# Decay and rate products of two pairs in one group on the row halves, and the first weight chunk sent in two cuts

## The chip, the cores and the metric

The kernel runs on one core of a Trainium2 chip. Its time is the device time of one execution in microseconds, the median of several runs. Engines are called as the profile calls them: PE is TensorE (PEld its weight load), DVE is VectorE, ACT is ScalarE, POOL is GpSimd, SP is SyncE, which here issues most of the DMAs.

## The reference

One trunk layer of a decoder in float32, for 256 prompt tokens and 8 sample tokens (264 columns, T in the kernel). D_MODEL is 2048, the feed-forward width 5504.

```python
x = x + 0.5 * swiglu(rmsnorm(x, n1), f1g, f1u, f1d)
proj = rmsnorm(x, nm) @ w_in            # 1536 columns of attention, 3328 of RWKV
o_att  = sliding-window attention with sinks (16 query heads, 4 key heads)
o_rwkv = rwkv_time_mix(proj[..., 1536:], ...)
x = x + concat(o_att, o_rwkv) @ w_out
x = x + 0.5 * swiglu(rmsnorm(x, n2), f2g, f2u, f2d)
y = rmsnorm(x, final_norm)

# in rwkv_time_mix; wl, al are 64 columns each of the shifted projection
w = -softplus(-(w0 + tanh(wl) @ w2)) - 0.5
logw = -exp(w)                          # decay
a = sigmoid(a0 + al @ a2)               # rate
kk = k * k_k;  k = k * (1 + (a - 1) * k_a);  kk = kk / norm(kk)
S, y = wkv_scan(S0, r, logw, k, v, kk, a)
```

## The kernel before

**Stages.** First feed-forward block (0 to 766 us of the profiled execution), mixing with the projection by `w_in` (766 to 1157), the rest of `w_out` (to 1271), second feed-forward block (to 1967), final norm.

**Weight products.** All big products go through `gemm` (L132). It walks the 128-row blocks of the inner dimension in chunks of CH = 4: `chunk` (L121) loads 128x512 float32 weights on SP into `raw` (ring of 6), copies them on ACT to `hi` (L128, a reduced float32 format, ring of 4), and subtracts on DVE into `lo` (L59 and L129, ring of 4). The activations are kept as pairs (`s`, `t`, `y`, `o`) of a high and a low part too. Three matmuls for each 128x128 block, `hi` by both parts and `lo` by the high part, 12 a chunk, add up in a PSUM tile `acc` (3 banks). All other products use PSUM tiles `m` (5 banks, `mp`, L118). With these the eight banks are taken.

**The order.** A list scheduler orders the instructions of each engine by its own model of time, inside the dependences, priorities (`tc.high_priority`) and pinned orders (`keep_in_program_order`). Between engines only semaphores order the work. Each engine works through its list in order, so an instruction that waits holds up all behind it.

**Start.** `first_ffn` (L290) loads `x0` on ACT's queue (the first 128 rows of x beside the norm gains), splits it, and asks for the first chunk of gate weights (L307) behind that split. Then come x's blocks 1 (on ACT's queue), 2 and 3 (on SP's). The first pass works chunk by chunk over eight PSUM banks.

**Mixing.** The 38 column blocks of `w_in` are produced in the order of SEQ (L38): two blocks of the low-rank inputs, then four batches of two pairs of heads, three blocks (r, k, v) to a pair; then keys and values, then queries. After each chunk, `gemm` calls `tick`, which advances each of the spawned tasks (generators) by one step. The first two blocks give `la` (128 rows: 64 of `wl`, 64 of `al`) and `sgl`, and `tw`, 65 rows: tanh of the first 64 of `la`, and a row of ones.

For each pair a task `prep` (L416) runs through: the decay product (`tw` by the pair's `ld` tile, 65 rows, the 65th carrying w0), the rate product (`la` by the other half of the `ld` tile, 128 rows of which the upper 64 are zero weights), each with its own PSUM tile `m`; Tanh of both on ACT; then Copy (`kk`) and Square on ACT; some steps later the norm product `m<-t,C`, whose result DVE inverts; a scan over the columns on DVE (L433); exponentials on ACT (`W`, `Wi`, and a short one to `XD`); and further products.

For each batch a task `chain` (the triangular solve and the passing of the state) follows: rounds of DVE instructions on `X`, `Xt` and `st`, transposes into `PT` and `TT` (L569 to L577), products `m<-PT,gm`, `m<-TT,W`, and so on; at its end each pair's output is normalised (squares, two products by `C`, a square root `t<-m,eps` on ACT, a reciprocal on DVE, L705) and gated by a product of `sgl` with another `ld` tile. ACT loads a set of function tables (ACT_TABLE_LOAD) ahead of an instruction whose function is not in the set that is loaded.

Names of tiles in profile rows: `tw`, `la`, `sgl`, `X`, `Xt`, `st`, `PT`, `TT`, `gm`, `kr`, `bk` as in the code; `ld` small loaded tiles; `t` temporaries (ring of NT = 16); `C` the constants; `vec` and `half` vectors of per-row parameters; `x`, `s` the input and its split.

Of the kernel before, what the change touches and what calls it, by code (L numbers as in the profile page):

```python
# [7 lines left out]
F32 = mybir.dt.float32  # L8
F32R = mybir.dt.float32r
AF = mybir.ActivationFunctionType  # L10
ALU = mybir.AluOpType
# [15 lines left out]
BATCH = [2, 2, 2, 2]  # L27
CH, NRAW, NHL = 4, 6, 4
NACC, NM = 3, 5
NS, NO, NY, NH, NT, NLD = 38, 8, 8, 40, 16, 6  # L30
NWARM = 11
NGM, NKR, NUV, NTT, NBT = 10, 5, 3, 2, 5
NSTEP = 4
# [6 lines left out]
PASS = [[0,1,2,3],[4,5,6,7],[8,9,10,11,12,13,14,15]]  # L40

VG1, VGM, VG2, VGF = 0, 16, 32, 48
VMU, VKK, VKA, VA0, VRK, VLW, VLB, VSK, VSD = 64, 90, 98, 106, 114, 122, 130, 138, 154
NVEC = 155
CID, CBO, CCM, CMK = 0, 128, 256, 384


def body(tc, I, O):
# [9 lines left out]
    def tt(e, out, a, b, op):  # L58
        return e.tensor_tensor(out=out, in0=a, in1=b, op=op)  # L59
# [40 lines left out]
    with ExitStack() as ctx:  # L100
# [17 lines left out]
        def mp():  # L118
            return pp.tile([P, 512], F32, tag="m", bufs=NM, name=uid("m"))

        def chunk(src, n, e, ahead=True):  # L121
            w = n * P
            with tc.high_priority() if ahead else nullcontext():
                raw = wp.tile([P, CH * P], F32, tag="raw", bufs=NRAW, name=uid("raw"))
                hi = wp.tile([P, CH * P], F32R, tag="hi", bufs=NHL, name=uid("hi"))
                lo = wp.tile([P, CH * P], F32R, tag="lo", bufs=NHL, name=uid("lo"))
                SP.dma_start(raw[:, :w], src)
                A.copy(hi[:, :w], raw[:, :w])  # L128
                tt(e, lo[:, :w], raw[:, :w], hi[:, :w].bitcast(F32), ALU.subtract)  # L129
            return hi, lo  # L130

        def gemm(ps, src, xs, step=None, rng=None, ahead=True, ready=None):  # L132
# [157 lines left out]
        def first_ffn(n2):  # L290
            def load(k0):
                return n1.split(xr[k0], True)

            def nxt(o):
                n2.split(xr[o])
                n2.square(xr[o])
                A.dma_start(xsp[o], xr[o])

            with tc.tile_pool(name="f1", bufs=1) as fp:
                cur[0] = (fp, NH)  # L300
                x0 = fp.tile([P, KD + T], F32, name="x0")
                A.dma_start(x0, I["x0"])
                n1 = Norm(VG1, gains=x0[:, 0:KD])
                xr = [x0[:, KD:]]
                at = load(0)
                with tc.issue_after(at.ins):
                    first = chunk(I["gu1"][0, 0][:, 0:CH * P], CH, V, False)  # L307
                for e, j0, j1 in ((A, 1, 2), (SP, 2, 4)):
                    xg = fp.tile([P, j1 - j0, T], F32, name=uid("x"))
                    e.dma_start(xg, I["xT"][:, j0:j1, :])  # L310
                    xr += [xg[:, j] for j in range(j1 - j0)]

                def more(q):
                    xg = fp.tile([P, 4, T], F32, tag="x", bufs=3, name=uid("x"))
                    tc.keep_in_program_order(A.dma_start(xg, I["xT"][:, q * 4:q * 4 + 4, :]))
                    xr.extend(xg[:, j] for j in range(4))

                ffn(n1, xr, I["gu1"], I["dn1"], nxt, load, more, None, first)
# [27 lines left out]
        def mixing_body(mx, n2, n3, XD, XR):  # L346
            def fix(shape, name):
                return mx.tile(list(shape), F32, name=name)
# [13 lines left out]
            G.memset(keep.rearrange("p (c t) -> p c t", c=4)[:, :, 0:1], 0.0)  # L362
            shc = fix((P, NSH, NB + 1), "shc")
            wc = fix((P, NPAIR, 4), "wc")
            tw = fix((65, T), "tw")
            G.memset(tw[64:65, :], 1.0)
            rs = fix((P, T), "rs")
            PJ = [fix((P, 268), f"pj{i}") for i in range(3)]
            for pj in PJ:
# [2 lines left out]
            unit = fix((P, 32), "unit")  # L372
            for i in range(4):
                G.tensor_copy(unit[i * 32:i * 32 + 32, :], ident[i * 32:i * 32 + 32, i * 32:i * 32 + 32])
            half = fix((P, 16), "half")
            ts(V, half, vec[:, VKA:VKA + 16], 0.5, ALU.mult)
            less = fix((P, 8), "less")
            ts(V, less, half[:, 0:8], -1.0, ALU.mult, 1.0, ALU.add)
            mu = vec[:, VMU:VMU + NSH]
# [32 lines left out]
            def c4(x):  # L412
                return x[:, :NP].rearrange("p (c t) -> p c t", c=4)

            def prep(p, bt, k, xrr, xk, xv):
                lw = load(I["lw"][p], (P, 256))  # L416
                zp = mp()
                mm(zp[:, :T], lw[0:65, 0:P], tw[0:65, :])
                ap = mp()
                mm(ap[:, :T], lw[:, P:2 * P], la)  # L420
                sg, a = tmp(), tmp()
                act(sg, zp[:, :T], AF.Tanh, scale=0.5)
                ts(G, sg, sg, 0.5, ALU.mult, 0.5, ALU.add)
                act(a, ap[:, :T], AF.Tanh, scale=0.5, bias=half[:, 8 + p:9 + p])
                kk, b = tmp(), tmp()
                act(kk, xk, AF.Copy, scale=vc(VKK + p))
                act(b, kk, AF.Square)
# [430 lines left out]
                odv[0] = od  # L858

            shifted(0, la)  # L860
            act(tw[0:64, :], la[0:64, :], AF.Tanh)
            shifted(1, sgl)
            act(sgl, sgl, AF.Tanh, scale=0.5)
            ts(G, sgl, sgl, 0.5, ALU.mult, 0.5, ALU.add)
# [156 lines left out]
def layout(i):  # L1021
# [3 lines left out]
    for n in (1, 2):  # L1025
# [10 lines left out]
    heads = np.array([(2 * p + h) * 4 + j for h in range(2) for p in range(2) for b in range(NB) for j in range(4)])  # L1036
    a["vec"] = c(np.concatenate([
        v(i["ffn1_norm"][0]), v(i["mix_norm"][0]), v(i["ffn2_norm"][0]), v(i["final_norm"]),
        v(i["shift_mu"][0][sc]), v(i["key_k"][0]), v(i["key_a"][0]), v(i["aaa_a0"][0]),
        v(i["bonus_r_k"][0].reshape(-1)), v(i["ln_x_w"][0]), v(i["ln_x_b"][0]),  # L1040
        np.broadcast_to(i["attn_sinks"][0], (P, 16)), i["attn_sinks"][0][heads][:, None]], 1))
    e64 = np.kron(np.eye(2), np.ones((64, 64)))
# [2 lines left out]
    a["cst"] = c(np.concatenate([np.eye(P), e64, np.eye(P) - e64 / 64,   # L1045
                                 np.concatenate([m, m], 0)], 1).astype(f4))
    a["shs"] = c(i["state_shift"][0][:, sc].reshape(NB, NSH, P).transpose(2, 1, 0))
    lw = np.zeros((8, P, 256), f4)
    lw[:, :64, :P] = i["decay_w2"][0].reshape(64, 8, P).transpose(1, 0, 2)
    lw[:, 64, :P] = i["decay_w0"][0].reshape(8, P)  # L1050
    lw[:, 64:, P:] = i["aaa_a2"][0].reshape(64, 8, P).transpose(1, 0, 2)
    a["lw"] = lw
    a["g2"] = c(i["gate_g2"][0].reshape(P, 8, P).transpose(1, 0, 2))
    bk = _buckets()
# [38 lines left out]
```

## Time and profile before

| what | value |
|---|---|
| median of 3 runs | 1982.49 us (1981.63 to 1985.6) |
| span of the profiled execution | 1978.1 us; its own time was not taken apart from the runs, which lie 4.4 us above the span by their median |
| instructions | 45244 |
| PE busy | 1962.6 us, 99% |
| DVE, ACT, POOL busy | 67%, 52%, 14% |
| DMA | 357.26 MB, mean 181 GB/s |

In the rows of the groups and of a timeline stands: the start in us (timeline only), busy time, engine, line, operation, output tile <- input tiles, shapes and types, the number of instructions taken together (x2), and in brackets the engine's idle time before and what ended it. The ends of PE's rows are modelled, so its spacing is read from starts.

### The profile page before, as it was taken

The page shows a single profiled execution, that of the slowest core. Times are in us where ns is not written, and L with a number is a line of the kernel's source. Part 1 is how long each engine was busy: PE and PEld are TensorE (multiplying, and loading weights), DVE is VectorE, ACT ScalarE, POOL GpSimd, SP SyncE. Part 2 cuts the span into 40 slices and gives each one's busy share as a digit, 9 for nine tenths or more (in the row PEclk, how much of TensorE's full clock was granted, in tenths as well). Part 3 has the DMA queues.
Part 4 walks back from the last instruction along what each step waited for, and adds up shares of the span by engine and source line. Part 5 has one row for each costly group of instructions (what it writes and reads, how often), then busy time and mean ns, then how long its engine had stood idle before and what let it go on. Part 6 is the DMA issues. An engine that isn't in the chain of part 4 may idle for free.

```text
span 1978.1 us, 45244 instructions
## 1 busy us (share of the span) xinstructions
PE 1962.6 (99%) x17011; PEld 1944.7 (98%) x17011; DVE 1318.0 (67%) x2591; ACT 1037.1 (52%) x2069; POOL 267.2 (14%) x382
## 2 busy tenths in 40 slices
PE   9999999999999999999999999999999999999998
PEld 9999999999999999999999999999999999999998
DVE  5865555655556567799988766866666666666655
ACT  5644444444444456666656754654444444444445
POOL 0401001010010113222211000210101001010012
PEclk9999999999999999999999999999999999999999
DMA  7565565655555567554545455565666566666654
GB/s 238 178 191 191 184 191 193 183 185 174 188 180 182 182 189 230 162 165 147 147 140 172 134 161 180 177 182 187 189 185 194 182 192 188 190 192 181 192 179 147
DMA packets 218875, 357.26 MB, mean 181 GB/s; under 512 B 33552, under 2 KB 72352, under 8 KB 218656
## 3 DMA queue, kind: packets, MB, share of 16 engines
q1 hardware_dynamic: 212144, 345.76, 56.1%
q10 hardware_dynamic: 6512, 8.61, 1.3%
q8 instruction: 133, 2.18, 0.4%
q14 instruction: 86, 0.70, 0.1%
HBM read 346.67 MB, written 9.69 MB: 180 GB/s over the span
## 4 chain that ended last, share of the span: by engine, by line
PE 96%; DVE 2%; DMA 1%; issue 1%; ACT 1%; SPq 0%; DVEq 0%; ACTq 0%
PE acc L75 88%; PE m L75 8%; DVE lo L59 0%; ACT t L69 0%; DMA x<-in_x 0%; DMA raw<-in_wout 0%; DVE y L59 0%; DVE st L59 0%; DVE Xt L59 0%; DMA sa<-gm 0%; DMA ld<-in_sT 0%; ACT hi L128 0%; PE m L505 0%; DVE t L705 0%; DVE gm L59 0%
## 5 line engine op out<-in xcount | busy, mean ns | idle before, releaser
L59 DVE TENSOR_TENSOR lo<-raw,hi 128x512 fp32r<-128x512 f32 (+1 forms) x1288 | 869.6, 679 | 526.9 <-ACT hi L128 504.5
L128 ACT CAST hi<-raw 128x512 fp32r<-128x512 f32 (+1 forms) x1288 | 777.4, 607 | 839.5 <-PE acc L75 766.0
L75 PE MATMUL acc<-s,hi 128*128 128x264 f32 x5940 | 1110.9, 286 | 2.3 <-DVE o L62 1.0
L75 PEld LDWEIGHTS acc<-s,hi 128*128 128x128 f32 x5940 | 923.4, 188 | 6.7 <-ACT hi L128 1.8
L75 PE MATMUL acc<-s,lo 128*128 128x264 f32 x2970 | 847.5, 286 | 0.5 <-DVE lo L59 0.5
L75 PEld LDWEIGHTS acc<-s,lo 128*128 128x128 f32 x2970 | 558.7, 188 | 2.2 <-DVE lo L59 0.9
L75 PE MATMUL acc<-t,hi 128*128 128x264 f32 x2752 | 502.8, 284 | 0.0
L75 PEld LDWEIGHTS acc<-t,hi 128*128 128x128 f32 x2752 | 426.0, 188 | 0.0
L75 PE MATMUL acc<-t,lo 128*128 128x264 f32 x1376 | 388.5, 284 | 0.0
L59 POOL TENSOR_TENSOR t<-t,t 128x264 f32<-128x264 f32 (+1 forms) x148 | 151.0, 1020 | 1146.6 <-ACT hi L128 789.4
L75 PEld LDWEIGHTS acc<-t,lo 128*128 128x128 f32 x1376 | 258.1, 188 | 0.0
L75 PE MATMUL acc<-y,hi 128*128 128x264 f32 x648 | 123.7, 284 | 0.0
L75 PEld LDWEIGHTS acc<-y,hi 128*128 128x128 f32 x648 | 101.2, 188 | 0.1
L75 PE MATMUL acc<-y,lo 128*128 128x264 f32 x324 | 91.9, 284 | 0.0
L59 DVE TENSOR_TENSOR t<-acc,t 128x264 f32<-128x264 f32 x156 | 67.4, 432 | 35.8 <-PE acc L75 35.5
L59 POOL TENSOR_TENSOR o<-o,o 128x264 f32<-128x264 f32 x43 | 35.8, 833 | 235.8 <-ACT o L69 231.8
L75 PE MATMUL acc<-o,hi 128*128 128x264 f32 x324 | 62.4, 282 | 0.0
L75 PEld LDWEIGHTS acc<-y,lo 128*128 128x128 f32 x324 | 60.8, 188 | 0.0
L69 ACT ACTIVATE t<-t 128x264 f32<-128x264 f32 (+1 forms) x110 | 46.6, 424 | 8.8 <-DVE t L433 5.5
L62 DVE SCALAR_TENSOR_TENSOR s<-acc,s 128x264 f32<-128x264 f32 x96 | 40.6, 427 | 15.5 <-PE acc L75 15.1
L75 PEld LDWEIGHTS acc<-o,hi 128*128 128x128 f32 x324 | 49.9, 188 | 0.0
L75 PE MATMUL m<-s,hi 128*128 128x264 f32 x260 | 47.9, 284 | 0.0
(261 smaller groups left out, 1283.5 us busy)
## 6 DMA issues: line engine op xcount, KB each, us to landing
raw<-in_gu SPq DMA_DIRECT2D x688, 256.0 KB, 3.3
raw<-in_dn SPq DMA_DIRECT2D x224, 256.0 KB, 2.8
raw<-in_win SPq DMA_DIRECT2D x152, 256.0 KB, 3.4
raw<-in_dn SPq DMA_DIRECT2D x160, 192.0 KB, 2.7
raw<-in_wout SPq DMA_DIRECT2D x64, 256.0 KB, 3.2
xsp<-x ACTq DMA_DIRECT2D x16, 132.0 KB, 3.4
s<-xsp SPq DMA_DIRECT2D x16, 132.0 KB, 4.0
ld<-in_sT SPq DMA_DIRECT2D x16, 128.0 KB, 2.9
```

The lines of the kernel that those rows point to most:

```text
L59: return e.tensor_tensor(out=out, in0=a, in1=b, op=op)
L62: return V.scalar_tensor_tensor(out=out, in0=a, scalar=s, in1=b, op0=op0, op1=op1)
L69: return A.activation(out=out, in_=in_, func=f, **k)
L75: return TE.matmul(out, lhsT, rhs, start=start, stop=stop, **k)
L128: A.copy(hi[:, :w], raw[:, :w])
```

## The change

- The decay and rate products of the two pairs of a batch are issued together, when the first pair's `prep` starts (`rates`). The `ld` tile of a pair is now 128x128: its upper 64 rows hold the decay weights, its lower 64 the rate weights. The decay product takes rows 0 to 63 of the array, the rate product rows 64 to 127.
- w0 no longer comes from a row of ones in `tw` (now 64 rows) but as the bias of Tanh; `vec` and `half` grow by 8 columns, and the memset of `tw`'s last row is gone.
- Each pair's Tanh outputs are kept in `bt.gates` until its `prep` takes them; the ring of `t` has 17 tiles.
- `chunk` takes cuts. For the first chunk of gate weights alone, the first 128 of 512 columns are loaded, cast and subtracted on their own, then the other 384.

```diff
--- before.py
+++ after.py
@@ -27,7 +27,7 @@
 BATCH = [2, 2, 2, 2]
 CH, NRAW, NHL = 4, 6, 4
 NACC, NM = 3, 5
-NS, NO, NY, NH, NT, NLD = 38, 8, 8, 40, 16, 6
+NS, NO, NY, NH, NT, NLD = 38, 8, 8, 40, 17, 6
 NWARM = 11
 NGM, NKR, NUV, NTT, NBT = 10, 5, 3, 2, 5
 NSTEP = 4
@@ -40,8 +40,8 @@
 PASS = [[0,1,2,3],[4,5,6,7],[8,9,10,11,12,13,14,15]]
 
 VG1, VGM, VG2, VGF = 0, 16, 32, 48
-VMU, VKK, VKA, VA0, VRK, VLW, VLB, VSK, VSD = 64, 90, 98, 106, 114, 122, 130, 138, 154
-NVEC = 155
+VMU, VKK, VKA, VA0, VW0, VRK, VLW, VLB, VSK, VSD = 64, 90, 98, 106, 114, 122, 130, 138, 146, 162
+NVEC = 163
 CID, CBO, CCM, CMK = 0, 128, 256, 384
 
 
@@ -118,15 +118,18 @@
         def mp():
             return pp.tile([P, 512], F32, tag="m", bufs=NM, name=uid("m"))
 
-        def chunk(src, n, e, ahead=True):
+        def chunk(src, n, e, ahead=True, cuts=None):
             w = n * P
+            cuts = [0, *(cuts or []), w]
             with tc.high_priority() if ahead else nullcontext():
                 raw = wp.tile([P, CH * P], F32, tag="raw", bufs=NRAW, name=uid("raw"))
                 hi = wp.tile([P, CH * P], F32R, tag="hi", bufs=NHL, name=uid("hi"))
                 lo = wp.tile([P, CH * P], F32R, tag="lo", bufs=NHL, name=uid("lo"))
-                SP.dma_start(raw[:, :w], src)
-                A.copy(hi[:, :w], raw[:, :w])
-                tt(e, lo[:, :w], raw[:, :w], hi[:, :w].bitcast(F32), ALU.subtract)
+                for c0, c1 in zip(cuts, cuts[1:]):
+                    c = slice(c0, c1)
+                    SP.dma_start(raw[:, c], src[:, c])
+                    A.copy(hi[:, c], raw[:, c])
+                    tt(e, lo[:, c], raw[:, c], hi[:, c].bitcast(F32), ALU.subtract)
             return hi, lo
 
         def gemm(ps, src, xs, step=None, rng=None, ahead=True, ready=None):
@@ -304,7 +307,7 @@
                 xr = [x0[:, KD:]]
                 at = load(0)
                 with tc.issue_after(at.ins):
-                    first = chunk(I["gu1"][0, 0][:, 0:CH * P], CH, V, False)
+                    first = chunk(I["gu1"][0, 0][:, 0:CH * P], CH, V, False, (P,))
                 for e, j0, j1 in ((A, 1, 2), (SP, 2, 4)):
                     xg = fp.tile([P, j1 - j0, T], F32, name=uid("x"))
                     e.dma_start(xg, I["xT"][:, j0:j1, :])
@@ -362,8 +365,7 @@
             G.memset(keep.rearrange("p (c t) -> p c t", c=4)[:, :, 0:1], 0.0)
             shc = fix((P, NSH, NB + 1), "shc")
             wc = fix((P, NPAIR, 4), "wc")
-            tw = fix((65, T), "tw")
-            G.memset(tw[64:65, :], 1.0)
+            tw = fix((64, T), "tw")
             rs = fix((P, T), "rs")
             PJ = [fix((P, 268), f"pj{i}") for i in range(3)]
             for pj in PJ:
@@ -372,8 +374,8 @@
             unit = fix((P, 32), "unit")
             for i in range(4):
                 G.tensor_copy(unit[i * 32:i * 32 + 32, :], ident[i * 32:i * 32 + 32, i * 32:i * 32 + 32])
-            half = fix((P, 16), "half")
-            ts(V, half, vec[:, VKA:VKA + 16], 0.5, ALU.mult)
+            half = fix((P, 24), "half")
+            ts(V, half, vec[:, VKA:VKA + 24], 0.5, ALU.mult)
             less = fix((P, 8), "less")
             ts(V, less, half[:, 0:8], -1.0, ALU.mult, 1.0, ALU.add)
             mu = vec[:, VMU:VMU + NSH]
@@ -412,16 +414,26 @@
             def c4(x):
                 return x[:, :NP].rearrange("p (c t) -> p c t", c=4)
 
+            def rates(p0, n):
+                ws = [load(I["lw"][p0 + j], (P, P)) for j in range(n)]
+                pre = [(mp(), mp()) for _ in range(n)]
+                for w, two in zip(ws, pre):
+                    for x, ps, r in zip((tw, la), two, HALF):
+                        mm(ps[:, :T], w[r, :], x[r, :])
+                out = []
+                for j, two in enumerate(pre):
+                    p = p0 + j
+                    sg, a = tmp(), tmp()
+                    for o, ps, c in zip((sg, a), two, (16, 8)):
+                        act(o, ps[:, :T], AF.Tanh, scale=0.5, bias=half[:, c + p:c + p + 1])
+                    ts(G, sg, sg, 0.5, ALU.mult, 0.5, ALU.add)
+                    out.append((sg, a))
+                return out
+
             def prep(p, bt, k, xrr, xk, xv):
-                lw = load(I["lw"][p], (P, 256))
-                zp = mp()
-                mm(zp[:, :T], lw[0:65, 0:P], tw[0:65, :])
-                ap = mp()
-                mm(ap[:, :T], lw[:, P:2 * P], la)
-                sg, a = tmp(), tmp()
-                act(sg, zp[:, :T], AF.Tanh, scale=0.5)
-                ts(G, sg, sg, 0.5, ALU.mult, 0.5, ALU.add)
-                act(a, ap[:, :T], AF.Tanh, scale=0.5, bias=half[:, 8 + p:9 + p])
+                if k == 0:
+                    bt.gates = rates(p, bt.n)
+                sg, a = bt.gates[k]
                 kk, b = tmp(), tmp()
                 act(kk, xk, AF.Copy, scale=vc(VKK + p))
                 act(b, kk, AF.Square)
@@ -858,7 +870,7 @@
                 odv[0] = od
 
             shifted(0, la)
-            act(tw[0:64, :], la[0:64, :], AF.Tanh)
+            act(tw, la[0:64, :], AF.Tanh)
             shifted(1, sgl)
             act(sgl, sgl, AF.Tanh, scale=0.5)
             ts(G, sgl, sgl, 0.5, ALU.mult, 0.5, ALU.add)
@@ -1036,7 +1048,7 @@
     heads = np.array([(2 * p + h) * 4 + j for h in range(2) for p in range(2) for b in range(NB) for j in range(4)])
     a["vec"] = c(np.concatenate([
         v(i["ffn1_norm"][0]), v(i["mix_norm"][0]), v(i["ffn2_norm"][0]), v(i["final_norm"]),
-        v(i["shift_mu"][0][sc]), v(i["key_k"][0]), v(i["key_a"][0]), v(i["aaa_a0"][0]),
+        v(i["shift_mu"][0][sc]), v(i["key_k"][0]), v(i["key_a"][0]), v(i["aaa_a0"][0]), v(i["decay_w0"][0]),
         v(i["bonus_r_k"][0].reshape(-1)), v(i["ln_x_w"][0]), v(i["ln_x_b"][0]),
         np.broadcast_to(i["attn_sinks"][0], (P, 16)), i["attn_sinks"][0][heads][:, None]], 1))
     e64 = np.kron(np.eye(2), np.ones((64, 64)))
@@ -1045,10 +1057,9 @@
     a["cst"] = c(np.concatenate([np.eye(P), e64, np.eye(P) - e64 / 64, 
                                  np.concatenate([m, m], 0)], 1).astype(f4))
     a["shs"] = c(i["state_shift"][0][:, sc].reshape(NB, NSH, P).transpose(2, 1, 0))
-    lw = np.zeros((8, P, 256), f4)
-    lw[:, :64, :P] = i["decay_w2"][0].reshape(64, 8, P).transpose(1, 0, 2)
-    lw[:, 64, :P] = i["decay_w0"][0].reshape(8, P)
-    lw[:, 64:, P:] = i["aaa_a2"][0].reshape(64, 8, P).transpose(1, 0, 2)
+    lw = np.zeros((8, P, P), f4)
+    lw[:, :64] = i["decay_w2"][0].reshape(64, 8, P).transpose(1, 0, 2)
+    lw[:, 64:] = i["aaa_a2"][0].reshape(64, 8, P).transpose(1, 0, 2)
     a["lw"] = lw
     a["g2"] = c(i["gate_g2"][0].reshape(P, 8, P).transpose(1, 0, 2))
     bk = _buckets()
```

## The prediction

> **What bounds the kernel now.** I read the page first: span, busy shares, the chain that ended last.
>
> ```profile
> span 1978.1 us, 45244 instructions
> PE 1962.6 (99%) x17011; PEld 1944.7 (98%) x17011; DVE 1318.0 (67%) x2591; ACT 1037.1 (52%) x2069; POOL 267.2 (14%) x382
> PE 96%; DVE 2%; DMA 1%; issue 1%; ACT 1%; SPq 0%; DVEq 0%; ACTq 0%
> ```
>
> TensorE is busy for 99% of the span and carries 96% of the chain, so a TensorE instruction taken away is worth its own spacing, and any new idle time of PE is lost. The span lies 4.4 us under the median of the runs (1982.49 - 1978.1); I make the sum against the span and add those 4.4 us back by quoting changes against 1982.5. The edits but one sit in the mixing stage, so next I read the windows there (columns after the window and its length: busy of PE, PE weight load, DVE, ACT, POOL, then granted clock, DMA share, GB/s).
>
> ```profile
> core 0: us, PE busy (x) PEld busy (x) DVE busy (x) ACT busy (x) POOL busy (x), PEclk, DMA share, GB/s
> 860.00:960.00 100.00, 98.24 (x1185) 93.80 (x1184) 91.19 (x255) 62.88 (x162) 27.25 (x53) 1.00 0.51 146
> 960.00:1060.00 100.00, 98.03 (x1157) 92.33 (x1152) 87.83 (x272) 56.33 (x139) 14.43 (x35) 1.00 0.47 138
> ```
>
> Here DVE stands at 91 and 88%: close behind PE, with its own serial chain (the scan rounds on X and Xt). PE is the bound, but a gain of PE in this stretch can run into DVE, and a pause of PE lets DVE catch up. The clock is full, so clocks play no part in the sum.
>
> **Part 1: the products of decay and rate.** In the tile view both kinds come 16 times, two instructions to a product: 8 products each. The timeline of PE prices one pair of them.
>
> ```profile
> L75 PE MATMUL m<-tw,ld x16: 383/386/490, 791.9 to 991.4; 65*128 65x264 f32 x16
> L75 PE MATMUL m<-la,ld x16: 383/384/388, 792.4 to 994.7; 128*128 128x264 f32 x16
> ```
>
> ```profile
> 811.50 0.61 PE L75 MATMUL m<-tw,ld 65*128 65x264 f32 x2
> 811.95 0.61 PE L75 MATMUL m<-la,ld 128*128 128x264 f32 x2
> 812.20 0.60 PE L75 MATMUL acc<-s,hi 128*128 128x264 f32 x2
> 812.64 0.28 PE L75 MATMUL acc<-s,lo 128*128 128x264 f32 x1
> 812.76 0.42 PE L75 MATMUL acc<-s,hi 128*128 128x264 f32 x2
> ```
>
> One weight product takes 0.12 us (812.64 to 812.76). From 811.50 to 812.64 lie both products of a pair and two weight products: 1.14 - 0.24 = 0.90, so 0.45 a product, 0.225 an instruction of 264 columns. Two pairs pay 1.80 us, the kernel 7.2 us. The 65 rows of tw cost as much as 128: rows left empty save nothing.
>
> The change puts tw's product on the upper 64 rows and la's on the lower 64. Whether two halves run side by side is shown by the existing products of kr and bk, 64 rows each, alternating between the halves:
>
> ```profile
> 826.36 0.63 PE L75 MATMUL m<-t,C 128*128 128x280 f32 x2
> 826.92 2.06 PE L75 MATMUL m<-kr,bk 64*128 64x128 f32 x32
> 828.90 0.39 PE L75 MATMUL acc<-s,hi 128*128 128x264 f32 x1
> 829.13 0.29 PE L75 MATMUL acc<-s,lo 128*128 128x264 f32 x1
> ```
>
> At 0.225 for 264 columns, 128 columns cost 0.109: 32 in a row would be 3.49 us, 16 slots of two 1.74. They took 1.98 (826.92 to 828.90), so the halves do run side by side. What is over is the price of going into the halves and out: 826.36 to 828.90 is 2.54; less 1.74 and less the two 280-column instructions (2 x 0.239) leaves 0.32, and the first weight product behind takes 0.23 instead of 0.12, 0.11 more. That is 0.32 to 0.43; I take 0.40.
>
> A group of the changed kernel has four products in two slots: 2 x 0.45 + 0.40 = 1.30 against 1.80, 0.50 saved, **2.0 us in four groups**. Bounds: 3.6 saved if nothing is paid for the switch (a gap that PE would have anyway), and 1.6 lost if these halves don't overlap. The built program does put each group's eight instructions together, with no weight product between, so one switch a group is right. The bias through Tanh instead of a 65th row, the smaller ld loads and the memset that goes are on ACT, SP and POOL, where PE doesn't wait for them; half the bytes of 8 small loads changes nothing, and I cost them at nothing. A group wants four of the five m banks at once; the releases it waits for in the built order (copies by ACT, a 128x8 sum on DVE) lie before it as they did. On SP both ld loads of a batch now stand together, one issue ahead of the weight loads behind them; the six raw tiles hide that. The t ring grows by one tile, since the second pair's rates live longer.
>
> **Part 1's side effect: activation tables.** With two pairs in one group, the second pair's rates are ready earlier, and its Square, Exp and Copy move forward in ACT's order. In batches 2 and 3 they now land between the two square roots (t<-m,eps) of an earlier batch's normalisation. Before:
>
> ```profile
> 917.56 0.62 ACT L128 CAST hi<-raw 128x512 fp32r<-128x512 f32 x1 [0.40 <-ACT t L403]
> 918.20 1.28 ACT L69 ACT_TABLE_LOAD   x1
> 919.50 0.48 ACT L69 ACTIVATE t<-m,eps 128x264 f32<-128x264 f32 x1
> 919.87 0.61 ACT L128 CAST hi<-raw 128x512 fp32r<-128x512 f32 x1
> 920.38 0.48 ACT L69 ACTIVATE t<-m,eps 128x264 f32<-128x264 f32 x1
> 927.25 0.51 ACT L69 ACTIVATE t<-t,vec 128x264 f32<-128x264 f32 x1
> 928.17 0.42 ACT L69 ACTIVATE t<-t 128x264 f32<-128x264 f32 x1
> ```
>
> One load, both roots. The built program of the changed kernel has: Copy (the row at 927.25), cast, Square (928.17), Exp, load, root, load, Exp, a short Exp, cast, load, root. By these rows, in the old clock: the cast ends near 918.2, Square and Exp to 919.0, first load and root to 920.8, second load and both Exp to 922.7, cast to 923.3, third load and root to 925.1. The second root frees an m bank, and in the new PE order the second pair's norm product m<-t,C, which takes that bank, stands eight weight products behind the second sgl product:
>
> ```profile
> 921.93 0.61 PE L75 MATMUL m<-sgl,ld 128*128 128x264 f32 x2
> 922.87 0.61 PE L75 MATMUL m<-tw,ld 65*128 65x264 f32 x2
> ```
>
> 921.93 + 0.45 + 7 x 0.12 = 923.2: PE arrives 1.9 us before the bank is free, and everything behind it on PE, weight products first, stands still. Today tw stands there and finds the bank free. The same order returns one batch later:
>
> ```profile
> 985.47 0.62 ACT L128 CAST hi<-raw 128x512 fp32r<-128x512 f32 x1 [0.22 <-ACT t L403]
> 986.11 1.28 ACT L69 ACT_TABLE_LOAD   x1
> 990.21 0.61 PE L75 MATMUL m<-sgl,ld 128*128 128x264 f32 x2
> 991.14 0.61 PE L75 MATMUL m<-tw,ld 65*128 65x264 f32 x2
> ```
>
> The same list from 985.47 puts the second root's end at 993.0 (67.9 us behind the first place) to 993.6 (the scan ahead of the Exp late by one 0.6 lo), PE's arrival at 991.2 to 991.8 (five to ten weight products behind the sgl product): 1.2 to 2.4, I take 1.9. **Together 3.8 us lost** (bounds: 0 if the pauses are given back by later waits, 5 if both reach 2.5). The casts behind come later by the loads too, but four hi tiles are in their ring and PE needs 12 x 0.12 = 1.45 for each, so I cost them at nothing as long as one chunk lies ready; without that cover a load's 1.28 would be paid at each place.
>
> A rule of the Trainium skill speaks harder against it: "ScalarE: Activation LUTs", What ACT_TABLE_LOAD costs, puts a drain of about 1380 ns on top of a load of about 1283 ns at every switch. The trace agrees with the load (1.28) and shows no drain: the load starts 0.02 us after the cast before it (917.56 + 0.62), the root 0.02 after the load. By the rule this case would be one of the rivals below.
>
> **Part 1 at the scan.** Before, PE stands 1.76 us in front of m<-PT,gm, whose true releaser is DVE's PT:
>
> ```profile
> 887.51 0.65 DVE L433 TENSOR_TENSOR_SCAN t<-keep,t 128x256 f32<-128x256 f32 x1
> 888.08 0.40 DVE L59 TENSOR_TENSOR PT<-X,unit 128x256 f32<-128x256 f32 x1
> 888.62 0.69 PE L75 MATMUL m<-PT,gm 32*32 32x32 f32 x32 [1.76 <-ACT t L69]
> ```
>
> The new order has the scan behind PT: PT comes 0.57 us earlier (888.08 - 887.51). **0.6 us gained**; 1.76 at most, nothing if PE's savings before it only make PE wait there longer.
>
> **Part 2: the first chunk in two cuts.** The start of the timeline:
>
> ```profile
> 5.24 0.51 ACT L69 ACTIVATE s<-x 128x264 fp32r<-128x264 f32 x1 [2.55 <-DMA x<-in_x]
> 5.66 0.60 ACT L128 CAST hi<-raw 128x512 fp32r<-128x512 f32 x1
> 6.29 0.69 DVE L59 TENSOR_TENSOR lo<-raw,hi 128x512 fp32r<-128x512 f32 x1
> 6.32 0.73 PE L75 MATMUL acc<-s,hi 128*128 128x264 f32 x2 [0.26 <-ACT hi L128]
> 7.52 1.65 ACT L128 CAST hi<-raw 128x512 fp32r<-128x512 f32 x3
> 8.60 0.65 PE L75 MATMUL acc<-s,hi 128*128 128x264 f32 x4
> ```
>
> A quarter cast, if its 0.60 shrinks with its columns to 0.15 to 0.3, lets the first product start 0.3 to 0.4 us before 6.32. But the chunk's 12 products take from 6.32 to 8.60, 2.28 us, against 12 x 0.12 = 1.45: PE is waiting for the splits of x and the casts, which run without a gap on ACT from 5.24 until past 7.52. The cut adds a cast, a subtraction and a DMA issue to that work and takes none away, so the end of the chunk stays where it is. The issue that SP makes more puts the x tiles and weight chunks behind it later by one issue; those wait in ACT's order anyway. I cost it at **0** (0.4 gained if the first product sets the pace, 0.5 lost if the added fixed costs fall on ACT's chain).
>
> **Sum.** -2.0 + 3.8 - 0.6 + 0 = +1.2 us: **1983.7 us**. About 0.2%, 4 us, is what a measurement of this kernel tells from no change; this is inside it.
>
> **Rivals.** The longest instruction in DVE's queue near the first place:
>
> ```profile
> 922.73 1.79 DVE L705 RECIPROCAL t<-t 128x264 f32<-128x264 f32 x1
> ```
>
> Given back: DVE at 91% is the second bound; while PE stands for the bank, DVE's rounds go on, and PE's later waits for DVE shrink by as much. Then the 3.8 goes: -2.6, **1979.9**. For it speaks the DVE share, against it that PE is still at 98%.
> All good ends: no switch cost (-3.6), the whole wait of 1.76 gone, the first product 0.4 earlier, pauses given back: -5.8, **1976.7**.
> It doesn't do what it says: the tw and la halves don't overlap and the switch is paid: +1.6 in place of -2.0, **1987.3**. Against it stand the kr,bk rows.
> Slower, at the scan: the second pair's Exp stands in ACT's queue before the first root and waits for DVE's scan, with the casts behind it. If DVE is late there by one such instruction (1.8 us), both roots and the bank come later by that at both places: 2 x 1.8 = 3.6 more, **1987.3**. It decides once DVE is more than the room of the casts behind; the 91% speaks for it, the early place of the scan in DVE's order against.
> Each table switch costs its load a second time: three loads ahead of the second root, at two places, 6 x 1.28 = 7.7 more, **1991.4**. The 0.02 us gaps speak against it.
>
> **How the numbers follow.** Forecast 0.40, given back 0.18, all good ends 0.14, no overlap 0.08, scan 0.19, double switch 0.01. Faster by over 0.2% (under 1978.5): the good ends, a third of the given-back case, a little of the forecast's tail: 0.22. Slower by over 0.2% (above 1986.5): nearly all of the last three less their shorter ends, 0.25. Within: 0.53. The range goes from halfway into the good ends, 1977.3, to 1988.0, past the two cases at 1987.3; outside stay half of the good ends and the long ends of the slow cases, under 0.2.
>
> **What would show it.** In the changed profile: the products of tw and la with 64 rows, eight instructions together, the next weight product some 1.3 us behind the group's start (0.9 + 0.89 would mean no overlap); 20 table loads of 1.28 instead of 16; a PE wait of 1 to 2.5 us at m<-t,C near 923 and 992 behind ACT's t<-m,eps; the wait at m<-PT,gm near 888 shorter; the first product near 5.95, and the second bank's first product no earlier than 8.60. I am wrong if PE shows no wait for the second root, if the stage from 766 to 1157 gains more than 3 us or loses more than 3, or if the start moves by over 0.5.

## The result and the profile after

The changed kernel takes 1987.24 us (median of 10 runs, 1985.5 to 1991.56), the one before 1983.36 in 10 runs of the same comparison (1978.27 to 1985.6): ratio 1.0032, 95% interval 1.0024 to 1.0040. By this ratio it is slower by 4.8 to 7.9 us, some 6. (The quotient of the two medians is smaller, 1.0020 or 3.9 us; the median of the kernel before lay between 1980.45 and 1983.36 in its four sets of runs.) The time lies inside the range of the prediction, but the forecast was "no change", and that was wrong.

The two profiles are not at the same place among their runs. A run lies 1.8 us above its span (1991.56 against 1989.8), so the profiled run of before was one of its quickest (1978.1 + 1.8), that of after one of its slowest; of the 11.7 us between the spans about half is spread. The page after:

```profile
span 1989.8 us, 45252 instructions
PE 1965.4 (99%) x17011; PEld 1944.9 (98%) x17011; DVE 1318.8 (66%) x2592; ACT 1042.5 (52%) x2074; POOL 259.3 (13%) x381
PE 93%; DVE 3%; ACT 1%; issue 1%; DMA 1%; SPq 0%; DVEq 0%; ACTq 0%
```

PE is as busy as it was, but the chain now runs through DVE and ACT for 4% in place of 3. The same two windows as before, and two short ones (granted clock in the third column from the right), with the row of before for 890 to 900 last:

```profile
860.00:960.00 100.00, 95.79 (x1091) 90.22 (x1090) 87.72 (x246) 61.66 (x153) 20.19 (x48) 0.97 0.48 138
960.00:1060.00 100.00, 91.88 (x1152) 85.95 (x1151) 84.37 (x262) 52.66 (x129) 13.38 (x39) 0.98 0.45 130
...
890.00:900.00 10.00, 10.00 (x83) 9.24 (x85) 7.28 (x12) 4.75 (x11) 0.68 (x3) 0.73 0.58 146
1030.00:1040.00 10.00, 6.46 (x54) 5.77 (x54) 6.82 (x29) 2.70 (x6) 0.99 (x3) 0.83 0.39 111
```

```profile
890.00:900.00 10.00, 10.00 (x137) 9.29 (x138) 9.51 (x19) 6.29 (x16) 3.17 (x6) 1.00 0.64 192
```

Two things are new. PE idles 12.3 us in these 200 (before 3.7), and the granted clock, full before, falls to half in places: in 890 to 900 PE is "busy" for all 10 us and gets 83 matmuls done, where before it did 137 (part of that is another mix of large and small products; the slow clock itself is priced below). The waits of PE say where (engine, output, releaser: total, times, longest):

```profile
PE m L75 <- ACT t L69: 3.6, 2, 2.0
PE acc L75 <- DVE lo L59: 3.2, 2, 2.9
PE m L75 <- DVE PT L59: 2.8, 2, 2.6
PE acc L75 <- DVE o L62: 1.3, 1, 1.3
```

The first line is the pair of waits for the roots that was predicted. ACT's timeline at the first place has the list as forecast, load, root, load, two Exp, cast, load, root, and PE waits for the second root at both places:

```profile
923.02 1.28 ACT L69 ACT_TABLE_LOAD   x1
924.31 0.48 ACT L69 ACTIVATE t<-m,eps 128x264 f32<-128x264 f32 x1
924.81 1.28 ACT L69 ACT_TABLE_LOAD   x1
926.10 0.42 ACT L69 ACTIVATE t<-t 128x256 f32<-128x256 f32 x1
926.43 0.19 ACT L69 ACTIVATE XD<-t 128x8 f32<-128x8 f32 x1
926.52 0.60 ACT L131 CAST hi<-raw 128x512 fp32r<-128x512 f32 x1
927.15 1.28 ACT L69 ACT_TABLE_LOAD   x1
928.44 0.48 ACT L69 ACTIVATE t<-m,eps 128x264 f32<-128x264 f32 x1
```

```profile
928.98 0.71 PE L75 MATMUL m<-t,C 128*128 128x264 f32 x2 [1.65 <-ACT t L69]
998.88 0.71 PE L75 MATMUL m<-t,C 128*128 128x264 f32 x2 [1.96 <-ACT t L69]
```

The second line of the waits was not predicted at all. At the last batch's solve DVE waits for the solve's data, which come back from DRAM, and a lo of the weights stands behind that wait in its list. The round stands two lo earlier than it did (behind 667 in halves_only, the changed kernel without the cut; behind 669 in before). DVE's first round, before and after, and PE after:

```profile
1024.48 0.19 DVE L59 TENSOR_TENSOR st<-X,Xt 128x30 f32<-128x30 f32 x1 [2.75 <-DMA Xt<-sa]
```

```profile
1032.56 0.19 DVE L59 TENSOR_TENSOR st<-X,Xt 128x30 f32<-128x30 f32 x1 [5.92 <-DMA Xt<-sa]
1034.00 0.68 DVE L59 TENSOR_TENSOR lo<-raw,hi 128x512 fp32r<-128x512 f32 x1
1034.74 0.39 PE L75 MATMUL acc<-s,lo 128*128 128x264 f32 x1 [2.94 <-DVE lo L59]
```

The third is the wait at 888, which grew from 1.76 us instead of shrinking, with the slow clock behind it: three weight products took 0.66 us from 890.27 on, where 0.37 is normal.

```profile
888.32 0.42 DVE L59 TENSOR_TENSOR PT<-X,unit 128x256 f32<-128x256 f32 x1
888.89 1.07 PE L75 MATMUL m<-PT,gm 32*32 32x32 f32 x32 [2.56 <-DVE PT L59]
890.27 0.64 PE L75 MATMUL acc<-s,hi 128*128 128x264 f32 x2
890.93 0.64 PE L75 MATMUL acc<-s,hi 128*128 128x264 f32 x2
```

### The profile page after: what moved, and what is told of

Read it like the earlier page. It is cut to its first block, busy times and chain, and to the rows that moved or that the text cites. A ratio compares the mean times of both kernels' runs of the same rounds, so it can differ in the third digit from the quotient of the medians.

```text
span 1989.8 us, 45252 instructions
## 1 busy us (share of the span) xinstructions
PE 1965.4 (99%) x17011; PEld 1944.9 (98%) x17011; DVE 1318.8 (66%) x2592; ACT 1042.5 (52%) x2074; POOL 259.3 (13%) x381
## 4 chain that ended last, share of the span: by engine, by line
PE 93%; DVE 3%; ACT 1%; issue 1%; DMA 1%; SPq 0%; DVEq 0%; ACTq 0%
PE acc L75 86%; PE m L75 7%; DVE lo L59 1%; ACT L69 0%; ACT t L69 0%; DVE Xt L59 0%; DVE st L59 0%; ACT hi L131 0%; DMA raw<-in_gu 0%; DMA Xt<-sa 0%; DVE y L59 0%; DVE t L717 0%; DVE t L62 0%; PE m L783 0%; DMA out_wkvp<-S 0%
## 5 line engine op out<-in xcount | busy, mean ns | idle before, releaser
L59 DVE TENSOR_TENSOR lo<-raw,hi 128x512 fp32r<-128x512 f32 (+2 forms) x1289 | 869.6, 678 | 530.3 <-ACT hi L131 506.4
L131 ACT CAST hi<-raw 128x512 fp32r<-128x512 f32 (+2 forms) x1289 | 777.9, 606 | 844.4 <-PE acc L75 756.3
L62 DVE SCALAR_TENSOR_TENSOR s<-acc,s 128x264 f32<-128x264 f32 x96 | 40.5, 427 | 15.5 <-PE acc L75 15.1
```

Source lines behind the costliest of these rows:

```text
L62: return V.scalar_tensor_tensor(out=out, in0=a, scalar=s, in1=b, op0=op0, op1=op1)
L131: A.copy(hi[:, c], raw[:, c])
```

## The experiments

To set kernels beside each other, I cut the mixing stage by PE's own weight products, from the 6001st to the 8101st of the trace, and split its length into PE's idle time (gaps between the rows), the time lost to the halved clock (half of each halved stretch in the clock record) and the rest, which is PE's own work. One profiled run each, so the clock column is one draw; the ratio is that of the timed runs to those of before. PE's own work spreads too: six builds with the same grouped halves (after, halves_only, roots_first, roots_later_solve, second_pair_later, halves_pool) have 382.1 to 384.2.

| kernel | ratio (95%) | stage | idle | halved clock | PE's work |
|---|---|---|---|---|---|
| before | 1 | 391.1 | 5.4 | 1.7 | 384.0 |
| after | 1.0032 (1.0024 to 1.0040) | 402.7 | 13.6 | 6.8 | 382.3 |
| cut_only | 0.9999 (0.9991 to 1.0008) | 393.3 | 7.6 | 1.7 | 384.1 |
| per_pair | 0.9996 (0.9988 to 1.0005) | 395.4 | 7.7 | 3.4 | 384.3 |
| halves_only | 1.0033 (1.0021 to 1.0044) | 398.6 | 13.0 | 3.4 | 382.1 |
| group_full | 1.0037 (1.0023 to 1.0050) | 398.9 | 10.7 | 3.4 | 384.8 |
| group01 | 1.0007 (0.9998 to 1.0016) | 393.5 | 6.6 | 3.4 | 383.5 |
| group23 | 1.0053 (1.0041 to 1.0066) | 402.2 | 15.5 | 5.1 | 381.5 |
| roots_first | 1.0033 (1.0021 to 1.0045) | 397.7 | 11.8 | 3.4 | 382.4 |
| roots_later_solve | 1.0041 (1.0029 to 1.0054) | 395.3 | 11.0 | 0.0 | 384.2 |
| second_pair_later | 1.0059 (1.0047 to 1.0072) | 406.3 | 12.5 | 10.2 | 383.5 |
| before_pool | 1.0041 (1.0029 to 1.0054) | 402.8 | 9.9 | 8.5 | 384.4 |
| halves_pool | 1.0061 (1.0048 to 1.0073) | 403.7 | 14.6 | 5.1 | 384.0 |
| per_pair_pool | 1.0025 (1.0014 to 1.0037) | 397.1 | 9.1 | 1.7 | 386.3 |

My theory after the result was that grouping the two pairs moves work in the lists of ACT and DVE, and that PE waits for it; first of all for the roots behind table loads. The rivals: the cut and the start, the halves themselves, and DVE's total work.

**cut_only.** The kernel before with the new `chunk` and this line:

```diff
-                    first = chunk(I["gu1"][0, 0][:, 0:CH * P], CH, V, False)
+                    first = chunk(I["gu1"][0, 0][:, 0:CH * P], CH, V, False, (P,))
```

> The kernel before with the first chunk sent in two cuts and nothing else. At the end of the start the changed kernel stands 0.4 to 0.7 us behind the one before. If that is the cut's own price, this kernel is 0.4 to 0.7 us slower (ratio 1.0003) and everything behind the start is as before; if the start was chance, no difference. Neither theory of the mixing stage (table loads, or later DVE) expects more than 1 us here.

1982.16 against 1982.01: nothing. The first product comes 0.93 us earlier than before's 6.32, and PE then waits for the splits of x, as in the timeline of this kernel:

```profile
5.39 0.49 PE L75 MATMUL acc<-s,hi 128*128 128x264 f32 x2
5.72 0.28 PE L75 MATMUL acc<-s,lo 128*128 128x264 f32 x1
6.37 0.39 PE L75 MATMUL acc<-s,hi 128*128 128x264 f32 x1 [0.37 <-ACT s L69]
6.96 0.39 PE L75 MATMUL acc<-s,hi 128*128 128x264 f32 x1 [0.19 <-DVE s L62]
```

The second accumulator's first product comes at 8.12 where before's comes at 8.60, and the mixing stage begins at 766.4 us (766.9 in before). In the profile of after it begins at 767.4; that later start was a matter of that run.

**halves_only.** The changed kernel without the cut (the line above undone).

> The changed kernel without the cut. If the loss lies in the mixing stage, this one is 5 to 6 us slower than before (ratio 1.0025 to 1.003), with 20 table loads and the two waits of 1.6 to 2 us at the norm products. If the later start is what shifts the mixing stage into longer waits, it comes out within 2 us of before.

1987.98 against 1982.01: the whole loss is here.

**per_pair.** Halves without cut and without grouping:

```diff
-                if k == 0:
-                    bt.gates = rates(p, bt.n)
-                sg, a = bt.gates[k]
+                sg, a = rates(p, 1)[0]
```

> Row halves without the cut and without the grouping: each pair's two products stand side by side, when its own prep starts; 16 table loads in the order of before. By the prediction's prices a pair takes 0.45 + 0.40 against 0.90, so 8 x 0.05 = 0.4 us faster, no difference that can be measured. Theory of the grouping (order of ACT and DVE): within 1 us of before. Theory that the halves themselves cost (switch, slower products, what stands behind them): slower by 3 us or more.

1981.43, no difference from 1982.01. The halves as such cost nothing that can be told; by this run and the last, the grouping does. This build has 18 table loads, not the 16 that were expected (two more at the last roots, near 1060), as have group01 and roots_first; so a load more is not by itself a loss.

**roots_first.** The second pair's Copy held behind the last root that was issued (shortened; `...` stands for what is left out):

```diff
-                act(kk, xk, AF.Copy, scale=vc(VKK + p))
+                i = act(kk, xk, AF.Copy, scale=vc(VKK + p))
+                if k and root[0]:
+                    tc.add_manual_dep(i.ins, root[0].ins.name, ...)   # order alone
...
-                act(r, vp[:, :T], AF.Sqrt, scale=1.0 / 64, bias=eps[:, 1:2])
+                root[0] = act(r, vp[:, :T], AF.Sqrt, scale=1.0 / 64, bias=eps[:, 1:2])
```

> The changed kernel without the cut, with the second pair's Copy, and so its Square and Exp, held behind the second root in ACT's order: 16 table loads again, no load between the roots. Theory of the tables: the two waits (3.6 us) and what they set off go, and the time is between 1 us faster and 2 us slower than before. Theory of the later DVE chain (long waits at PT,gm and near 1034, and halved clock behind them): the loss stays at 4 us or more.

1988.60: no better than with the loads between the roots. The two waits for the roots are gone from its list (3.4 us in halves_only), the wait for lo is not:

```profile
PE acc L76 <- DVE lo L60: 3.4, 2, 3.2
PE m L76 <- DVE PT L60: 3.0, 2, 2.6
PE m L76 <- ACT t L70: 1.4, 1, 1.4
PE acc L76 <- DVE Xt L60: 1.3, 1, 1.3
```

The stage is only 0.9 us shorter than in halves_only, and the second feed-forward block, where PE never idles, 2.3 us longer (see the end). So the table loads explain two waits, but taking them away lowers the idle time by 1.2 us and not by 3.4, and does not give the time back; my first theory falls short.

**group01 and group23.** The condition `if k == 0` of the grouping taken only for `bt.i < 2`, or only for `bt.i >= 2`; the other batches as in per_pair.

> Row halves without the cut; two pairs in one group in batches 0 and 1 only, pair by pair in batches 2 and 3, so 16 table loads in the order of before. The products of the two groups are 0.8 to 1.0 us shorter. Theory that DVE's solve takes it back: the wait at m<-PT,gm near 888 grows from 1.8 to about 2.6 us and the time stays within 0.5 us of before (1981.5 to 1982.5). Theory that the gain is kept: the wait stays at 1.8 and the time falls by 0.8 to 1.0 us.

1981.96 against 1980.45, no difference that can be told. PE's work falls by 0.6 to 0.9 us against cut_only and per_pair, and the wait at 888 takes it back:

```profile
PE m L75 <- DVE PT L59: 2.6, 1, 2.6
```

> The other half: pair by pair in batches 0 and 1, grouped in batches 2 and 3. Theory that the order in the later batches costs the time (table loads between the roots at the first place, and the last solve's first round standing one weight chunk earlier in DVE's list): 3 to 6 us slower than before, with a wait of 1.6 to 2 us at m<-t,C near 925, and the wait at 888 at 1.8. Theory that the grouping as such costs (four banks at once, switches): half of the loss here, half in the run of batches 0 and 1.

1992.37, ratio 1.0053: more than the loss of all four. Its waits:

```profile
PE m L75 <- ACT TT L613: 4.9, 1, 4.9
PE acc L75 <- DVE o L62: 2.2, 1, 2.2
PE m L75 <- DVE PT L59: 2.2, 1, 2.2
PE m L75 <- ACT t L69: 2.0, 2, 1.6
```

Of the root waits one is left, of 1.6; the 4.9 ends at 1034.6, where the last solve begins, and has no like of its length in the other builds. So grouping in batches 0 and 1 alone costs nothing that can be told and grouping in batches 2 and 3 alone does; but this loss is not made of the same waits as that of the changed kernel, so the run does not show which of them is the cause.

**group_full.** The kernel before with the four products of two pairs in one group, as matmuls of 65 and 128 rows over the whole array.

> Four products of two pairs in one group, but on the whole array as before (65 and 128 rows); no cut. Same order of ACT and DVE as the changed kernel. If the halves run side by side, PE's own work in the mixing stage is some 1.7 to 2 us more than in the run of row halves alone, and the time 0 to 2 us above its 1988.0, so 1988 to 1990; if halves bring nothing, PE's work and the time equal that run's.

1988.16. PE's work is 2.6 us more than in halves_only, and the rows of a group agree:

```profile
882.62 0.61 PE L75 MATMUL m<-tw,ld 65*128 65x264 f32 x2
...
884.64 0.28 PE L75 MATMUL acc<-s,lo 128*128 128x264 f32 x1
```

From the group's start to this lo, less two weight products of 0.12, are 1.78 us, with halves 1.25 (the rows are in the first point of the next section). So the halves do run side by side; but PE idles 2.3 us less, and the time is the same. What the halves save, PE spends waiting.

**roots_later_solve.** roots_first with the last solve issued later: `DWAIT = (11, 11, 11, 3)` becomes `(11, 11, 11, 15)`.

> The second pair held behind the roots (16 table loads, 1988.6 before this edit), and the last batch's solve sent to the schedule 12 chunks later, which puts its first round two weight chunks later in DVE's list (behind the 670th lo instead of the 668th; before: 669th). Theory that lo instructions behind the DMA wait of that first round stop PE: the wait of 3.2 us at acc<-s,lo near 1031 goes, and the time is 1984 to 1986.5. Theory that DVE's total work sets the stage: the wait moves elsewhere and the time stays at 1987.5 to 1989.5.

1990.56 (1984.47 to 1991.38). The wait for lo is down to 0.4, as meant, but others have come, and the time did not fall:

```profile
PE m L76 <- ACT t L789: 1.9, 1, 1.9
PE m L76 <- ACT TT L613: 1.8, 1, 1.8
...
PE m L847 <- DVE t L67: 1.1, 1, 1.1
```

**second_pair_later.** halves_only, with the second pair's Copy in batches 2 and 3 two steps later and behind the last cast (shortened):

```diff
+                late = k == 1 and bt.i > 1
+                if late:
+                    yield from pause(2)
-                act(kk, xk, AF.Copy, scale=vc(VKK + p))
+                i = act(kk, xk, AF.Copy, scale=vc(VKK + p))
+                if late:
+                    tc.add_manual_dep(i.ins, his[-1 - 0].ins.name, ...)   # order alone
```

> Row halves and grouped products in all batches, no cut; in batches 2 and 3 the second pair's Copy, and so its Square, Exp and all its work on DVE, comes two steps later and is held behind the last cast issued by then: 16 table loads, and the second pair's work behind both roots, near its old place. Theory that the early work of the second pair costs the time: the time falls to 1983 or less (before: 1980.5 to 1982.0), with less than 9 us of idle PE in the mixing stage (13.0 in the run of row halves alone). Theory that the four products at one place, with four banks, cost it: 1986 or more.

1994.27: worse than any other. A miss for the theory of the early second pair in this form, though not a test of the old order: holding one instruction moved the solves of batches 1 and 2 as well (PT of batch 1 stands behind the 644th lo in DVE's list, before behind the 640th), and beside the wait at 888 (2.56) three more of 2.5 to 3.1 us came up, each of the four with a halved clock around its end.

**Three runs with subtractions on POOL.** In the blocks of `w_in` from the ninth on, the third of the four lo goes to POOL:

```diff
-                hi, lo = ready or chunk(src[:, k0 * P:k1 * P], k1 - k0, V, ahead)
+                hi, lo = ready or chunk(src[:, k0 * P:k1 * P], k1 - k0, G if k0 == other else V, ahead)
...
-            gemm(ps, I["win"][t], n2.xs, tick)
+            gemm(ps, I["win"][t], n2.xs, tick, other=8 if t > 7 else None)
```

> The kernel before with one of four lo subtractions of the w_in blocks from the ninth on moved from DVE to POOL: 30 x 0.6 = 18 us off DVE in the mixing stage. Theory that DVE bounds this stage beside PE: idle PE there falls from 5.4 to 7.6 us to 4 or less and the time by 1 to 4 us, to 1977 to 1980.5. Theory that only single waits count: no change or slower, since POOL is slower at it.

> The run of row halves alone (grouped, no cut) with the same 30 subtractions on POOL. If DVE is what takes the gain of the halves back, its idle PE falls from 13.0 to 8 or less, and the gap to the same edit of the kernel before, 6 us without the edit, shrinks to 2 us or less or turns into a gain of up to 2. If the grouping costs by itself (banks, switches, loads), the gap stays at 4 to 6 us.

> The run of row halves pair by pair, with the same 30 subtractions on POOL. Pair by pair costs nothing without the edit, so this one lies within 1 us of the kernel before with the edit, by either theory; it is the version that could beat both kernels, if the edit helps.

1990.42, 1994.70 and 1987.20 against 1982.46: all slower. The theory of DVE's total work missed in the first two, and both theories in the third, which is 3 us below the first. But these runs do not test that theory, because the edit did not take work off DVE: its busy time in the stage rose, from 324.2 to 330.0 us in before_pool against before, and by 4.5 us in each of the other two against the same build without the edit. A lo took 1.36 to 1.37 us on POOL and 0.68 on DVE, and beside it DVE instructions got longer. In before_pool, POOL first, then DVE, and the same DVE instruction in before:

```profile
823.47 1.29 POOL L59 TENSOR_TENSOR lo<-raw,hi 128x512 fp32r<-128x512 f32 x1 [1.49 <-ACT hi L128]
823.59 1.47 DVE L62 SCALAR_TENSOR_TENSOR t<-t,vec,t 128x264 f32<-128x264 f32 x1
```

```profile
823.26 0.49 DVE L62 SCALAR_TENSOR_TENSOR t<-t,vec,t 128x264 f32<-128x264 f32 x1
```

In the stage 24, 23 and 24 DVE instructions took over 0.5 us more than the shortest of their kind, all beside work on POOL, and 23, 19 and 23 of the 30 lo there had one beside them; in the three builds without the edit there were 1, 0 and 0. So whether DVE's total work sets this stage stays open; that the order of the lists does is argued, not shown. The gap between grouped and not grouped is 4.3 us with this edit (1994.70 to 1990.42).

No version here beats the kernel before by more than its interval.

## Why the prediction was wrong

- **The products (-2.0): right.** PE's work in the stage fell by 1.7 us in the profiles (384.0 to 382.3), which is no more than its spread among builds, and by 2.6 against the same grouping on the whole array. The rows are firmer. The eight instructions of this group start 7 ns apart in twos:

```profile
882.12 0.49 PE L75 MATMUL m<-tw,ld 64*128 64x264 f32 x1
882.12 0.49 PE L75 MATMUL m<-la,ld 64*128 64x264 f32 x1
...
882.95 0.38 PE L75 MATMUL m<-la,ld 64*128 64x264 f32 x1
883.27 0.51 PE L75 MATMUL acc<-s,hi 128*128 128x264 f32 x2
883.61 0.29 PE L75 MATMUL acc<-s,lo 128*128 128x264 f32 x1
```

  882.12 to 883.27 is 1.15 us, where 1.30 was predicted; the two weight products behind take 0.34 in place of 0.24, so the group costs 1.25. Against 1.78 on the whole array that is 0.53 saved, 2.1 us in four groups.
- **The roots (+3.8): right as waits, not shown as a cost.** 1.65 + 1.96 = 3.6, by the mechanism named. But roots_first, without these waits, has only 1.2 us less idle time than halves_only and is no faster. That is nearer to the bound of 0 that the prediction gave this term ("if the pauses are given back by later waits") than to 3.8. The 20 loads are there, and between a load and its neighbours lie again 0.01 to 0.03 us; the drain of 1380 ns that the Trainium skill adds at a switch ("ScalarE: Activation LUTs", What ACT_TABLE_LOAD costs) is not in this trace either.
- **The wait at 888 (-0.6): wrong in sign, +0.8.** The scan did move behind PT, but PT came no more than 0.3 us earlier relative to the start of the stage, and PE, which got there 1.1 us earlier (shorter groups, and five weight products fewer ahead of the place), simply stood there longer (1.76 to 2.56). The prediction named this mechanism as the lower bound of the term, but put it at nothing, where it costs as much as PE had saved before. In group01, with two groups ahead of it, the wait is 2.59.
- **The start (0): right as far as the times tell**, by cut_only. The signs given for it missed: the first product came 0.93 us earlier and not 0.4, and the second accumulator's at 8.12 and not from 8.60 on.
- **The last solve: missing from the sum.** I followed the edits' own instructions through the lists as far as the second root and not to the next place where DVE waits for a DMA. One wait of 2.9 us (3.3 in halves_only) came there, where the profile of before has none over 0.4. Not all of it is a loss, though: cut_only and per_pair, which are as fast as before, have a wait of 2.1 and 2.5 us a few us later, in front of `m<-BT,W`, which after has not.
- **"The clock is full, so clocks play no part in the sum": wrong.** It was full in the two windows quoted, and not in the whole stage: before's own profile has 3.4 us at half clock, from 1088.8 on. After a wait of 2 to 3 us the granted clock was halved in 11 of 18 cases, for 3.4 or 6.8 us, which costs half of that again. Over the timed runs this can be read without one profile's luck: the mean granted clock of the 53 runs of before that carry one is 0.9966, that of the 10 runs of after 0.9956; in the comparison of halves_only it is 0.9952 against 0.9964. 0.001 of 1988 is 2.0 us, a third of the 6 us.

So the steps that failed are the gain at 888, which was a loss, the waits behind the second root, which were left out, and the clock, which was put at nothing. Worked out afterwards from the table, against cut_only and per_pair, the sum is -2 for the products, some 6 more of idle (13.6 against 7.6 and 7.7: 3.6 roots, 0.8 at 888, the rest at the last solve and in small waits) and 2 of clock: +6. This is bookkeeping and not a proof of the causes. The sign of the forecast's middle was right and its size a fifth. The stage from the 6001st to the 8101st weight product lost 7.5 us in halves_only and 11.6 in after against before, far over the 3 us that the prediction gave as a sign of being wrong.

Among the rivals, the slower one (ACT held at DVE's scan) did not occur at the first place, where ACT has no such wait. At the second it did in a small form: the Exp ahead of both roots waited 0.47 us for the scan (L445), where 1.8 was feared. At 890, where the scan was moved behind PT, ACT's Exp waited 4.92 us for it (3.37 in before), but no cast behind it came too late for PE.

```profile
992.48 0.42 ACT L69 ACTIVATE t<-t 128x256 f32<-128x256 f32 x1 [0.47 <-DVE t L445]
```

What stays open is why the time doesn't come back when the root waits are taken away; the runs show other waits in their place, of 1 to 3 us, but not a rule for where they come up.

## What to carry to other kernels

Where two engines and a dozen tasks are interleaved by a scheduler, cost an edit by the order it leaves behind: take the built program, and walk PE's list against ACT's and DVE's through the whole stage, not only at the edit. A gain of a few tenths on the bounding engine is kept only if nothing it meets next is late; ask for every saving which wait comes next. And price a wait of PE at more than its length: where the halved clock came with it, one of 2 to 3 us cost 1.7 to 3.4 us more here. When work is moved to another engine, read the first engine's busy time in the new profile before concluding anything: here 30 instructions left DVE, and its busy time rose.

## What was not expected of the hardware

- **Short waits halve the clock.** In the 14 profiles, all eight waits of PE of 2.8 us or more in the mixing stage had the clock halved around their end, and eight of the fifteen between 2.1 and 2.6 us; 1.76 us did it in cut_only and not in before, at the same place. Waits are not the only occasion: six of the 28 halved stretches in the stage (the one of before, at 1088.8, and its like in after, per_pair, group01, before_pool and halves_pool) began with no gap of PE over 0.1 us in the 6.8 us ahead of them, behind a run of small products (`m<-S,PT`, `m<-kr,S`, `m<-qb,ld`). Why was not tried. In the windows of halves_only the wait at 888 (2.56 us) leaves the clock full, the one at 1031 (3.28) does not:

```profile
890.00:900.00 10.00, 10.00 (x126) 8.95 (x126) 9.36 (x19) 7.20 (x19) 3.00 (x8) 1.00 0.66 183
1026.00:1036.00 10.00, 6.32 (x49) 5.54 (x48) 6.43 (x27) 2.70 (x6) 0.99 (x3) 0.71 0.41 113
```

  The halved stretches are 3.41 us long or twice that. The Trainium skill ("TensorE: Matmul & The Clock Gate", Part 1) describes a free-running window of 3413 ns over which the activity of PE is counted; the trace agrees with the length, and a window at a chance place fits that the same wait does it in one run and not in the next. The Trainium skill's advice to keep gaps under about 3 us ("TensorE: Matmul & The Clock Gate", Why this matters for your kernels) is too mild here: 1.8 to 2.6 us were enough in about half of the cases.
- **The same weight products run at different speeds in different builds.** In the second feed-forward block, with no idle and a full clock, 5400 weight products took 656.5 us (before, cut_only, per_pair), 656.2 (halves_only, after) and 658.5 (roots_first); in the first block 656.4 in these six. Four other builds are slower there too: roots_later_solve with 657.3, before_pool and per_pair_pool with 657.7, halves_pool with 658.8. So 0.8 to 2.3 us of what these five lose lie in a block that no edit touched. In roots_first the products that read the t tiles kept their spacing (121.7 to 122.0 ns); those that read the o tiles with lo went from 120.6 to 126.1 ns, and the five times more numerous ones that read the s tiles with lo from 121.7 to 123.4. Where the tiles lie may be the cause; that was not tried.
